# Pools of one PSUM slot each, and modulation sums hung behind named DVE instructions

## The chip, the core and the metric

The kernel runs on one core of one Trainium2 chip. The metric is the device time of one execution in microseconds; lower is better.

## The reference, cut to what matters

Two transformer blocks run one after the other over 1024 tokens of width 1024, all in float32. Each block takes six modulation vectors from a conditioning vector, mixes the tokens, and ends in a gated feed-forward network with a small convolution between its up-projection and its gate.

```python
def first_block(x, c, w_mod, b_mod, ...):
    mod = (silu(c) @ w_mod + b_mod)[:, None, :]
    sh1, sc1, g1, sh2, sc2, g2 = split(mod, 6)
    h = _rms(x, norm1_w) * (1 + sc1) + sh1
    ...                                     # state-space layer and windowed attention
    x = x + g1 * (mixed @ w_out)
    h2 = _rms(x, norm2_w) * (1 + sc2) + sh2
    return x + g2 * _conv_ffn(h2, w_up, conv_w, conv_b, w_down)

def _conv_ffn(h, w_up, conv_w, conv_b, w_down):
    up = causal_depthwise_conv(h @ w_up, conv_w) + conv_b     # width 3, 2 x 2816 columns
    val, gate = split(up, 2)
    return (silu(gate) * val) @ w_down

def second_block(x, c, ctx, c_ctx, ada_w, ada_b, ...):
    mx = split((silu(c) @ ada_w + ada_b)[:, None, :], 6)
    mc = split(silu(c_ctx) @ ada_w + ada_b, 6)
    ...                                     # recurrent, convolutional and spatial mixers
    x_new = layer_norm(ALPHA * x + mx[2] * (mix_x @ w_out), ln1_g, ln1_b)
    ffn_x = conv_ffn(modulate(x_new, mx[3], mx[4]), ffn_up, ffn_conv_w, ffn_conv_b, ffn_down, rows)
    return layer_norm(ALPHA * x_new + mx[5] * ffn_x, ln2_g, ln2_b)
```

`c` is one vector, so a modulation vector is one row times a 1024 x 1024 matrix.

## The kernel before

The products are float32 accuracy out of three reduced ones: each operand is split into a high part (`wh`, `gh`, a cast on ACT) and a low part (`wl`, `gl`, a subtraction on POOL or DVE, line 147 or 143), and three matmuls add high x high, high x low and low x high into one PSUM accumulator.

A planner sets the order of the work. The program is written in one order; the planner simulates it and gives every engine its own queue, in which an instruction stands where its inputs and its buffer are ready in that simulation, earlier written work first. On the chip each queue then runs strictly in that order. Tiles come from pools; a tile with `bufs=n` takes one of n slots when one is free. A pool that is opened over the space of a closed one waits for it.

PSUM has eight banks. `psum` (line 88) opens a set of pools by role and closes the set before; `pt` (line 100) takes a tile of a role. A role in capitals takes two banks a slot (1024 columns), one in small letters one bank. The sets that matter here: up-projection of block 1 `U=2, y=2, v=1, m=1` (line 1307), of block 2 `U=3, y=1, v=1` (line 1693), both down-projections `d=8` (line 1160), the start of block 2 `lv=2, tp=1, o=1` and `z=4` (lines 1315, 1316).

**Up-projection** (`up_proj`, line 1036). 22 pairs p, each a column tile of `val` and the one of `gate` that belongs to it. Pairs 0 to 2 are `plain`: four products of 24 matmuls. Pairs 3 to 21 are `seven` (line 1117): the 2 x 2 block product of a pair with seven half-size products instead of eight, 84 matmuls in all, on sums of weights made by POOL (`prep`, line 1092) and on sums of activations T1 to T4. DVE adds the seven results up, in lines 1126, 1128, 1130, 1133 and 1135, into `gt` (gate half) and back into the PSUM tile U (value half). `act` then runs the convolution of the pair before: in block 1 `gate1` (line 1247; DVE line 1257, ACT line 1255), in block 2 `gate2` (line 1276), and ACT's queue stores the result to DRAM. The raw weights come over SP's queue (line 122) into three buffers.

**Down-projection** (`down_proj`, line 1158). Two column halves; in each, eight accumulators `ps_d`, one for each tile of tokens, take 11 steps q of 48 matmuls (six a tile). `load` (line 1170) brings the weights of a step, multiplies them by the gate row (DVE, line 1175), splits them (POOL), and brings and splits two stored tiles (`gl`, DVE line 147). Steps 0 and 1 of the first half are loaded at high priority and run for six accumulators first and then for the last two; `slots` is the order of the accumulators. At the end of the first half DVE adds each accumulator to the residual (`put`, line 1196), which frees it for the second half.

**Modulation sums.** What the later stages need of the modulation vectors is computed beside the feed-forward network of block 1. `mod_half` (line 287) makes 512 columns of one vector: eight loads of 128 x 512 weights (`mw`, two buffers, SP, line 293) and eight DVE instructions (lines 296 and 298) that add each times its scalar into `macc`. Then small matmuls (lines 209 and 228, into role `m`) sum over the partitions, and DVE adds the bias. It is a generator that yields after each of the eight:

```python
        for k in range(KT):
            t = pool.tile([P, 512], F32, tag="mw", name="mw", bufs=2)
            nc.sync.dma_start(t, self.a[w][k * P:(k + 1) * P, o:o + 512])
            ...
                v.scalar_tensor_tensor(acc, t, s, acc, op0=ALU.mult, op1=ALU.add)
            if k < KT - 1:
                yield
```

`mods_up` makes ten such halves, 80 sums, for the up-projection, which asks for four or five after each pair from the third on (line 1151); `mods_down` makes six halves, 48 sums, and the down-projection asks for three after each `load` (line 1226). Nothing ties a sum to a place but that it is written there.

Of the kernel before, what the change touches and what calls it, by code (L numbers as in the profile page):

```python
# [19 lines left out]
F32 = mybir.dt.float32  # L20
# [4 lines left out]
ALU = mybir.AluOpType  # L25
AX = mybir.AxisListType

P = 128
D = 1024
# [5 lines left out]
PLAIN = 3  # L35
# [30 lines left out]
class Net:  # L66
# [21 lines left out]
    def psum(self, layer=0, **roles):  # L88

        for k in sorted(self.psctx, reverse=True):
            if k >= layer:
                self.psctx.pop(k).close()
        self.psctx[layer] = es = self.es.enter_context(ExitStack())
        for r, n in roles.items():
            pool = es.enter_context(self.tc.tile_pool(name="ps_" + r, bufs=1, space=bass.MemoryType.PSUM))
            self.psn[r] = (pool, n)

    def pt(self, role, *shape):  # L100
        if callable(role):
            return role(*shape)
        n = 1024 if role.isupper() else 512
        pool, bufs = self.psn[role]
        return pool.tile(list(shape) or [P, n], F32, tag=role, name="ps_" + role, bufs=bufs)
# [39 lines left out]
    def split_on(self, eng, hi, lo, x):  # L145
        self.nc.scalar.copy(hi, x)  # L146
        eng.tensor_sub(lo, x, hi.bitcast(F32))  # L147
# [139 lines left out]
    def mod_half(self, w, part, vec, half, acc, pool):  # L287

        nc, v = self.nc, self.nc.vector
        o = part * D + half * 512  # L290
        for k in range(KT):
            t = pool.tile([P, 512], F32, tag="mw", name="mw", bufs=2)
            nc.sync.dma_start(t, self.a[w][k * P:(k + 1) * P, o:o + 512])
            s = self.cact[:, vec * 8 + k:vec * 8 + k + 1]
            if k == 0:
                v.tensor_scalar(acc, t, s, None, op0=ALU.mult)
            else:
                v.scalar_tensor_tensor(acc, t, s, acc, op0=ALU.mult, op1=ALU.add)  # L298
            if k < KT - 1:
                yield  # L300

    def mods_up(self, role):

        for w, part, vec, to, bias in self.MODS_UP:
            for half in range(2):
                acc = self.mpool.tile([P, 512], F32, tag="macc", name="macc", bufs=1)
                yield from self.mod_half(w, part, vec, half, acc, self.mpool)
                self.mod_put(to, half, acc, bias, vec, role)
                yield

    def mods_down(self, accs, pool):

        self.sums = []
        for w, part, vec, to, bias in self.MODS_DOWN:
            for half in range(2):
                acc = accs[:, len(self.sums)]
                self.sums.append((to, half, acc, bias, vec))
                yield from self.mod_half(w, part, vec, half, acc, pool)
                yield
# [715 lines left out]

    def up_proj(self, up, act_fn, g_dr, step, mods):
# [80 lines left out]
        def seven(p):  # L1117
# [8 lines left out]
            v.tensor_add(u2, u2, y)  # L1126
            self.mm_half(z, b, 0, *T3, stop=False)
            v.tensor_add(u4, u2, z)
            self.mm_half(Z, b, 512, *T1, stop=False)
            v.tensor_add(gt[:, 512:1024], u4, Z)  # L1130
            self.mm_half(X, c, 0, *B21, start=False)
            self.mm_half(z, c, 512, *T4, start=False)
            v.tensor_add(gt[:, 0:512], u2, z)
            self.mm_half(Z, d, 0, *B22, start=False)
            v.tensor_add(Z, u2, Z)
# [6 lines left out]
        for p in range(NF):  # L1142
# [8 lines left out]
            for _ in range(4 + p % 2 if p >= PLAIN else 0):  # L1151
                next(step, None)
# [5 lines left out]
    def down_proj(self, down, gate, g_dr, x_dr, setup, done, slots, alpha, mods):  # L1158
# [9 lines left out]
        NQ = NF // 2  # L1168

        def load(nh, q):  # L1170
# [4 lines left out]
            v.tensor_tensor(r2, r2, gh, op=ALU.mult)  # L1175
            self.split_on(nc.gpsimd, *w, r)
            hs = []
            for p in (2 * q, 2 * q + 1):
# [3 lines left out]
                self.split_on(v, h, l, r)  # L1182
# [21 lines left out]
        for nh in range(2):  # L1204
            ps = [self.pt("d") for _ in range(NT)]
            if nh == 0:
# [12 lines left out]
                step = self.mods_down(accs, pool) if mods else iter(())  # L1219
            late = NQ - 3 if nh else NQ  # L1220
            for q in range(0 if nh else 2, late):
# [4 lines left out]
                for _ in range(3):  # L1226
                    next(step, None)
# [588 lines left out]
```

## Time and profile before

| what | value |
|---|---|
| median of 3 runs (lowest, highest) | 2737.31 us (2733.43, 2741.5) |
| the profiled execution: time, span | 2739.78 us, 2737.6 us |
| mean granted clock of TensorE | 0.94 |
| PE busy | 2468.7 us (90%) |
| DVE busy | 1803.5 us (66%) |
| ACT busy | 997.3 us (36%) |
| POOL busy | 1247.3 us (46%) |
| matmuls | 11558 |

The span runs from the first to the last instruction. PE is TensorE, DVE VectorE, ACT ScalarE, POOL GpSimd, SP the engine whose queue issues most transfers. An engine's busy time is the time in which it runs an instruction; what it waits for is named by the engine and line that released it. A clock of 1.00 is the full rate of 2.4 GHz, 0.5 is 1.2 GHz.

### The profile page before, as it was taken

The numbers are of one execution on the slowest core, as the hardware profiler recorded it, in microseconds if no ns is written. First come the engines' busy times: TensorE is split into PE (matmuls) and PEld (weight loads), VectorE is DVE, ScalarE is ACT, GpSimd is POOL, SyncE is SP. The second block draws the span as 40 slices with busy tenths as digits, with TensorE's granted clock in tenths as the row PEclk, the third lists the DMA queues.
The fourth block names the chain that finished last, engine by engine and source line by source line (L and its number), as shares of the span: only waits on it lengthen the run. The fifth ranks groups of instructions, "written<-read, shape, count | busy, mean of one in ns | idle before, by whom it ended". The sixth has DMA issues, their size and how long they took to land.

```text
span 2737.6 us, 31230 instructions
## 1 busy us (share of the span) xinstructions
PE 2468.7 (90%) x11558; PEld 2008.6 (73%) x11558; DVE 1803.5 (66%) x2634; ACT 997.3 (36%) x1470; POOL 1247.3 (46%) x769
## 2 busy tenths in 40 slices
PE   7999989888889979799999878997988999997998
PEld 3777777667768868587777767876766888875886
DVE  8479566877885575645146767677877777775545
ACT  4324543342234432224216446453243333332221
POOL 3353341566667841122123445345345777761222
PEclk9999799999999999899899989999999999998999
DMA  6522124234442256644121101123311222235442
GB/s 240 153 60 59 39 96 189 70 116 146 150 138 74 92 183 217 213 147 145 49 70 54 35 16 51 35 74 117 145 54 61 70 93 78 84 138 185 148 151 86
DMA packets 119017, 295.72 MB, mean 108 GB/s; under 512 B 24145, under 2 KB 38273, under 8 KB 118865
## 3 DMA queue, kind: packets, MB, share of 16 engines
q1 hardware_dynamic: 112528, 270.66, 30.1%
q10 hardware_dynamic: 6336, 23.07, 2.2%
q8 instruction: 91, 1.49, 0.2%
q14 instruction: 62, 0.50, 0.1%
HBM read 243.19 MB, written 49.31 MB: 107 GB/s over the span
## 4 chain that ended last, share of the span: by engine, by line
PE 59%; DVE 20%; DMA 9%; issue 5%; ACT 4%; POOL 3%; SPq 0%; DVEq 0%; POOLq 0%; ACTq 0%
PE ps_d L1192 14%; PE ps_U L1033 11%; PE ps_g L160 8%; PE ps_Z L160 5%; PE ps_v L1033 5%; DMA mw<-in_ada_w 4%; PE ps_z L160 3%; PE ps_y L1033 3%; DVE macc L298 2%; DVE cv L1257 2%; PE ps_lv L1588 2%; DVE cv L1276 1%; DVE gl L147 1%; DVE wl L143 1%; PE ps_s L606 1%
## 5 line engine op out<-in xcount | busy, mean ns | idle before, releaser
L147 POOL TENSOR_TENSOR wl<-wr,wh 128x512 fp32r<-128x512 f32 (+1 forms) x158 | 282.0, 1795 | 543.3 <-ACT wh L146 515.1
L1033 PE MATMUL ps_U<-a,wh 128*128 128x512 f32 x1216 | 386.6, 400 | 12.2 <-ACT u L1124 8.7
L1192 PE MATMUL ps_d<-wh,gh 128*128 128x512 f32 x704 | 278.0, 395 | 53.9 <-DVE cv L1276 24.7
L1033 PEld LDWEIGHTS ps_U<-a,wh 128*128 128x128 f32 x1216 | 233.6, 193 | 63.2 <-ACT u L1124 9.7
L1192 PE MATMUL ps_d<-wh,gl 128*128 128x512 f32 x704 | 276.3, 393 | 3.3 <-DVE gl L147 3.3
L1192 PE MATMUL ps_d<-wl,gh 128*128 128x512 f32 x704 | 277.4, 394 | 0.0
L160 PE MATMUL ps_g<-wh,a 128*128 128x512 f32 (+1 forms) x768 | 245.8, 400 | 25.9 <-ACT wh L141 11.8
L1033 PE MATMUL ps_U<-a,wl 128*128 128x512 f32 x608 | 241.0, 398 | 1.4 <-POOL wl L147 1.4
L160 PE MATMUL ps_Z<-a,wh 128*128 128x512 f32 x704 | 230.4, 405 | 4.6 <-DVE vs L1380 4.6
L1276 DVE SCALAR_TENSOR_TENSOR cv<-ps_U,cols,cv 128x945 f32<-128x945 f32 (+2 forms) x176 | 213.8, 1219 | 27.3 <-ACT cv L1268 24.4
L147 POOL TENSOR_TENSOR wl<-S,wh 128x512 fp32r<-128x512 f32 (+1 forms) x114 | 201.4, 1780 | 32.8 <-ACT wh L146 32.8
L146 ACT CAST gh<-rx 128x1024 fp32r<-128x1024 f32 x88 | 89.4, 1046 | 340.7 <-PE ps_d L1192 130.6
L1192 PEld LDWEIGHTS ps_d<-wh,gh 128*128 128x128 f32 x704 | 134.0, 190 | 83.9 <-issue 55.9
L160 PEld LDWEIGHTS ps_g<-wh,a 128*128 128x128 f32 x768 | 149.4, 202 | 59.6 <-ACT wh L141 12.9
L147 DVE TENSOR_TENSOR gl<-rx,gh 128x1024 fp32r<-128x1024 f32 x88 | 127.6, 1480 | 51.7 <-ACT gh L146 51.7
L160 PEld LDWEIGHTS ps_Z<-a,wh 128*128 128x128 f32 x704 | 134.6, 194 | 31.1 <-issue 5.0
L1192 PEld LDWEIGHTS ps_d<-wh,gl 128*128 128x128 f32 x704 | 133.9, 190 | 31.9 <-DVE gl L147 4.1
L160 PE MATMUL ps_g<-wl,a 128*128 128x512 f32 (+1 forms) x384 | 152.6, 398 | 4.4 <-POOL wl L143 2.9
L143 POOL TENSOR_TENSOR wl<-wr,wh 128x1024 fp32r<-128x1024 f32 x35 | 92.5, 2644 | 140.5 <-ACT wh L141 140.3
L1192 PEld LDWEIGHTS ps_d<-wl,gh 128*128 128x128 f32 x704 | 134.1, 190 | 28.5 <-issue 0.9
L146 ACT CAST wh<-S 128x512 fp32r<-128x512 f32 (+1 forms) x114 | 84.2, 762 | 190.8 <-POOL S L1108 133.2
L146 ACT CAST wh<-wr 128x512 fp32r<-128x512 f32 (+1 forms) x158 | 112.6, 736 | 104.7 <-PE ps_v L1033 36.5
(526 smaller groups left out, 5827.9 us busy)
## 6 DMA issues: line engine op xcount, KB each, us to landing
mw<-in_ada_w SPq DMA_DIRECT2D x112, 256.0 KB
wr<-in_w_up SPq DMA_DIRECT2D x44, 512.0 KB
rx<-g_w_up SPq DMA_DIRECT2D x44, 512.0 KB
wr<-in_f_up SPq DMA_DIRECT2D x44, 512.0 KB
rx<-g_f_up SPq DMA_DIRECT2D x44, 512.0 KB
g_w_up<-cv ACTq DMA_DIRECT2D x22, 512.0 KB
wr<-in_w_down SPq DMA_DIRECT2D x22, 512.0 KB
g_f_up<-cv ACTq DMA_DIRECT2D x22, 512.0 KB
```

Of the source, the lines that this page charges most:

```text
L143: (self.nc.gpsimd if self.turn else self.nc.vector).tensor_sub(lo, x, hi.bitcast(F32))
L146: self.nc.scalar.copy(hi, x)
L147: eng.tensor_sub(lo, x, hi.bitcast(F32))
L160: self.nc.tensor.matmul(out, a, b, start=i == 0, stop=i == n - 1)
L298: v.scalar_tensor_tensor(acc, t, s, acc, op0=ALU.mult, op1=ALU.add)
L606: nc.tensor.matmul(ps[:, gp, 1:P], wc[o:o + 64, r, gp, 1:9].rearrange("p k h -> p (k h)"), st[o:o + 64, r, gp, 0:P - 1], start=False, stop ...
L1033: self.nc.tensor.matmul(out, a, b, start=start and i == 0, stop=stop and i == 11, skip_group_check=True)
L1192: nc.tensor.matmul(ps, a[:, sl], b, start=q == 0 and j == 0, stop=q == NQ - 1 and j == 5, skip_group_check=True)
L1257: v.scalar_tensor_tensor(t[:, s:], us[part][:, :L - s], wt(j), t[:, s:], op0=ALU.mult, op1=ALU.add)
L1276: v.scalar_tensor_tensor(ov, s[:, r0 + di:r1 + di, c0 + dj:c1 + dj], wt(3 * (di + 1) + dj + 1), ov, op0=ALU.mult, op1=ALU.add)
L1588: nc.tensor.matmul(ps[:, j], ck(kk)[:, j], ck(qq)[:, j], start=True, stop=True)
```

## The change

Three things are changed. `psum` opens n pools of one slot for a role of n slots, and `pt` takes them in turn. `mod_half` loads the weights of sum k+1 right after it has written sum k, one step ahead of their use, and yields ahead of each sum; the extra yields of its callers go. And the generator is no longer advanced after a pair or a load: `behind` advances it right after one DVE instruction is written and tells the planner that what this puts on DVE may not be queued ahead of that instruction (it sets no wait, and it does not bind transfers, ACT or PE). The instructions are the four adds of each pair, a fifth in every fourth pair, and in the down-projection the weight product and the two `gl` of each `load`.

```diff
@@ def psum
         for r, n in roles.items():
-            pool = es.enter_context(self.tc.tile_pool(name="ps_" + r, bufs=1, space=bass.MemoryType.PSUM))
-            self.psn[r] = (pool, n)
+            self.psn[r] = cycle([es.enter_context(self.tc.tile_pool(name=f"ps_{r}{j}", bufs=1, space=bass.MemoryType.PSUM))
+                                 for j in range(n)])
@@ def pt
-        pool, bufs = self.psn[role]
-        return pool.tile(list(shape) or [P, n], F32, tag=role, name="ps_" + role, bufs=bufs)
+        return next(self.psn[role]).tile(list(shape) or [P, n], F32, tag=role, name="ps_" + role, bufs=1)
@@ def mod_half
+        def load(k):
+            t = pool.tile([P, 512], F32, tag="mw", name="mw", bufs=2)
+            nc.sync.dma_start(t, self.a[w][k * P:(k + 1) * P, part * D + half * 512:part * D + half * 512 + 512])
+            return t
+
+        t = load(0)
         for k in range(KT):
-            t = pool.tile([P, 512], F32, tag="mw", name="mw", bufs=2)
-            nc.sync.dma_start(t, self.a[w][k * P:(k + 1) * P, o:o + 512])
+            yield
             s = self.cact[:, vec * 8 + k:vec * 8 + k + 1]
             if k == 0:
                 v.tensor_scalar(acc, t, s, None, op0=ALU.mult)
             else:
                 v.scalar_tensor_tensor(acc, t, s, acc, op0=ALU.mult, op1=ALU.add)
             if k < KT - 1:
-                yield
+                t = load(k + 1)
@@ def mods_up, def mods_down
-                yield
@@ new
+    def behind(self, ins, step):
+
+        with self.tc.issue_after(ins.ins):
+            next(step, None)
@@ def seven
-            v.tensor_add(u2, u2, y)
+            self.behind(v.tensor_add(u2, u2, y), step)
             self.mm_half(z, b, 0, *T3, stop=False)
-            v.tensor_add(u4, u2, z)
+            self.behind(v.tensor_add(u4, u2, z), step)
             self.mm_half(Z, b, 512, *T1, stop=False)
-            v.tensor_add(gt[:, 512:1024], u4, Z)
+            self.behind(v.tensor_add(gt[:, 512:1024], u4, Z), step)
...
-            v.tensor_add(gt[:, 0:512], u2, z)
+            self.behind(v.tensor_add(gt[:, 0:512], u2, z), step)
             self.mm_half(Z, d, 0, *B22, start=False)
-            v.tensor_add(Z, u2, Z)
+            ins = v.tensor_add(Z, u2, Z)
+            if p % 4 == 0:
+                self.behind(ins, step)
@@ the loop over pairs
-            for _ in range(4 + p % 2 if p >= PLAIN else 0):
-                next(step, None)
@@ def load, in down_proj
-            v.tensor_tensor(r2, r2, gh, op=ALU.mult)
+            self.behind(v.tensor_tensor(r2, r2, gh, op=ALU.mult), step)
...
-                self.split_on(v, h, l, r)
+                self.behind(self.split_on(v, h, l, r), step)
@@ the loop over steps
-                for _ in range(3):
-                    next(step, None)
```

## Rows read from the trace of the kernel before

**Rows 1.** Busy time by stretch: us, each engine's busy time (instructions), clock, DMA share, GB/s.

```profile
core 0: us, PE busy (x) PEld busy (x) DVE busy (x) ACT busy (x) POOL busy (x), PEclk, DMA share, GB/s
577.90:829.70 251.80, 218.07 (x909) 174.97 (x909) 203.04 (x190) 76.51 (x101) 161.31 (x98) 0.93 0.43 142
829.70:982.90 153.20, 153.20 (x674) 125.90 (x673) 84.20 (x81) 62.64 (x80) 124.23 (x80) 1.00 0.24 79
...
1018.00:1128.80 110.80, 110.80 (x480) 91.60 (x481) 63.69 (x61) 25.21 (x25) 20.92 (x8) 0.98 0.66 219
1128.80:1160.80 32.00, 11.62 (x49) 8.71 (x48) 20.58 (x23) 6.08 (x6) 4.78 (x2) 0.81 0.61 199
...
2114.20:2437.90 323.70, 323.70 (x1430) 268.11 (x1429) 237.02 (x239) 115.74 (x154) 237.03 (x170) 1.00 0.24 80
...
2483.60:2490.00 6.40, 6.33 (x15) 5.01 (x16) 1.23 (x1) 1.06 (x1) 0.00 (x0) 0.51 0.29 97
2490.00:2693.00 203.00, 203.00 (x897) 168.12 (x897) 89.33 (x68) 53.28 (x55) 52.82 (x18) 1.00 0.44 147
```

**Rows 2.** Groups of DVE's instructions, 577.9 to 829.7: count, busy, mean ns, idle before.

```profile
L298 DVE SCALAR_TENSOR_TENSOR macc<-mw,cact,macc 128x512 f32<-128x512 f32 x66 | 83.1, 1259 | 38.2 <-DMA mw<-in_ada_w 30.8 <-DMA mw<-in_w_mod 6.8
...
L296 DVE TENSOR_SCALAR macc<-mw,cact 128x512 f32<-128x512 f32 x9 | 7.6, 840 | 0.0
```

**Rows 3.** What PE waited for, 577.9 to 829.7: us in total, times, longest.

```profile
PE ps_m L209 <- DVE macc L298: 14.6, 5, 4.1
PE ps_U L1033 <- ACT u L1124: 8.7, 3, 4.6
```

**Rows 4.** Groups of PE's instructions, 577.9 to 829.7: the sums' own matmuls.

```profile
L209 PE MATMUL ps_m<-ones,macc 128*128 128x1 f32 x64 | 9.0, 252 | 14.6 <-DVE macc L298 14.6
...
L228 PE MATMUL ps_m<-macc,ones 128*1 128x512 f32 x4 | 2.0, 590 | 0.0
```

**Rows 5.** Timeline at the first down-projection's start, DVE and PE: start, us, instruction, idle before.

```profile
1001.66 3.48 DVE L147 TENSOR_TENSOR gl<-rx,gh 128x1024 fp32r<-128x1024 f32 x3
...
1016.51 1.27 DVE L1257 SCALAR_TENSOR_TENSOR cv<-ps_U,cols,cv 128x1022 f32<-128x1022 f32 x1
...
1017.93 0.77 PE L1192 MATMUL ps_d<-wh,gh 128*128 128x512 f32 x1 [12.13 <-DVE cv L1257]
```

**Rows 6.** Timeline at the second down-projection's start, DVE and PE.

```profile
2456.24 2.34 DVE L147 TENSOR_TENSOR gl<-rx,gh 128x1024 fp32r<-128x1024 f32 x2
...
2468.18 1.22 DVE L147 TENSOR_TENSOR gl<-rx,gh 128x1024 fp32r<-128x1024 f32 x1
...
2477.22 6.29 DVE L1276 SCALAR_TENSOR_TENSOR cv<-ps_U,cols,cv 128x1008 f32<-128x1008 f32 x5
...
2483.66 0.76 PE L1192 MATMUL ps_d<-wh,gh 128*128 128x512 f32 x1 [24.66 <-DVE cv L1276]
```

**Rows 7.** What PE waited for, 1115 to 1180.

```profile
PE ps_d L1192 <- DVE a L1201: 17.1, 1, 17.1
```

**Rows 8.** Timeline of DVE inside the first down-projection: two sums.

```profile
1111.01 1.90 DVE L298 SCALAR_TENSOR_TENSOR a<-mw,cact,a 128x512 f32<-128x512 f32 x1 [1.77 <-DMA mw<-in_ada_w]
...
1125.46 2.42 DVE L298 SCALAR_TENSOR_TENSOR a<-mw,cact,a 128x512 f32<-128x512 f32 x2 [5.38 <-DMA mw<-in_ada_w]
```

**Rows 9.** Timeline at the start of block 2, DVE, ACT and PE.

```profile
1299.63 1.22 DVE L143 TENSOR_TENSOR wl<-wr,wh 128x1024 fp32r<-128x1024 f32 x1
...
1309.01 0.56 ACT L380 ACTIVATE hT<-ps_d,mod_sh_a,mod_sc_a 128x256 f32<-128x256 f32 x1 [0.32 <-PE ps_d L379]
...
1309.97 0.78 PE L160 MATMUL ps_z<-wh,a 128*128 128x512 f32 x1
```

**Rows 10.** Groups of DVE's instructions, 1018 to 1160.8: the sums of line 298.

```profile
L298 DVE SCALAR_TENSOR_TENSOR a<-mw,cact,a 128x512 f32<-128x512 f32 x42 | 38.5, 916 | 48.1 <-DMA mw<-in_ada_w 47.7
```

**Rows 11.** Timeline of PE ahead of pair 0 of block 1.

```profile
496.42 0.48 PE L379 MATMUL ps_s<-ident,xn 128*128 128x128 f32 x1 [7.00 <-DVE xn L348]
```

**Rows 12.** What SP's queue waited for, 829.7 to 982.9.

```profile
SPq L122 <- POOL wl L147: 148.6, 15, 19.6
```

More of the change, by code (lines that the diff above doesn't have):

```diff
@@ L146, in split_on @@
         self.nc.scalar.copy(hi, x)
-        eng.tensor_sub(lo, x, hi.bitcast(F32))
+        return eng.tensor_sub(lo, x, hi.bitcast(F32))
     def gate_row(self, i):
@@ L289, in mod_half @@
         nc, v = self.nc, self.nc.vector
-        o = part * D + half * 512
+        def load(k):
[3 more added lines that the diff above has]
+        t = load(0)
         for k in range(KT):
-            t = pool.tile([P, 512], F32, tag="mw", name="mw", bufs=2)
-            nc.sync.dma_start(t, self.a[w][k * P:(k + 1) * P, o:o + 512])
+            yield
             s = self.cact[:, vec * 8 + k:vec * 8 + k + 1]
@@ L318, in mods_down @@
                 yield from self.mod_half(w, part, vec, half, acc, pool)
-                yield
     def mods_end(self, ps):
@@ L1168, in down_proj @@
         NQ = NF // 2
+        step = iter(())
         def load(nh, q):
@@ L1218, in down_proj @@
                     accs = self.act.tile([P, KT, 512], F32R, tag="a16", name="a16", bufs=4).bitcast(F32)
-                step = self.mods_down(accs, pool) if mods else iter(())
+                    step = self.mods_down(accs, pool)
             late = NQ - 3 if nh else NQ
```

## The prediction

> **What bounds the kernel now.** I read the busy time by stretch first, then what DVE and PE wait for where PE is not full, then the timelines at the edges. In most stretches PE is never idle at a granted clock of 1.00: eight late pairs of the first up-projection take 153.2 us, 19.15 a pair, and 17 pairs of the second block's 19.04 each [rows 1]. So time can be won only where PE stands, and the change touches four such places.
>
> First, the ten pairs before those eight (from pair 3 on, where `seven` begins, 84 matmuls each) take 251.8 us, 25.2 a pair, PE busy 218.1 at clock 0.93 [rows 1]. What sets them apart is the modulation sums: 75 of the 80 that the first up-projection does run here (66 on line 298, 9 on line 296), 90.7 us of DVE, and DVE stands 37.6 us for their weights [rows 2]. With 203.0 us busy [rows 1] that is 240.6 of 251.8: DVE is the bound. In the eight late pairs it is busy 84.2 us, 10.5 a pair [rows 1]. The generator is asked for 4 or 5 sums a pair, but the planner, for which a load has landed sooner than it does, issues 7.5. PE's own waits are the consequence: 14.6 us of the sums' matmuls for the sum, 8.7 for ACT's copy of the first product, which stands behind DVE's convolution [rows 3].
>
> Second, between the first up-projection and its down-projection PE stands 12.13 us, released by DVE's last read of pair 21's U (line 1257, start 1016.51) [rows 5]. By the addresses of the kernel before, the accumulator that is written first lies in bank 0, which pair 20 held and left 20 us earlier; so the one pool of eight waits as a whole. The same edge in block 2 costs 24.66 us [rows 6], and then 6.4 us at clock 0.51 [rows 1]. Third, inside the first down-projection 32.0 us pass with 49 matmuls, where 10.9 would do (203.0/897 x 48) [rows 1]: PE waits 17.1 us for DVE's evacuation of line 1201 [rows 7], which is queued behind weight products and sums that wait up to 5.4 us for a load [rows 8]. Fourth, the first `z` of block 2 starts at 1309.97, when ACT has read the last `ps_d` (1309.01 plus 0.56) [rows 9].
>
> **The change part by part.** Nothing is computed more or less: sums, loads, matmuls and evacuations keep their number and change their place.
>
> *Sums in the up-projection.* 81 calls of the generator hang on the 81 places that the 19 pairs offer, 4 or 5 a pair. DVE's demand becomes 10.5 + 90.7/19 = 15.3 us of 19.15; in the late pairs it was idle 8.6 a pair, so 4.8 go into 8.6. Behind each sum on DVE stand the next add, which frees `z` for PE, and the convolution; block 2 runs such pairs with DVE 13.9 of 19.04 busy and PE full [rows 1]. The next load leaves a whole step before its sum; with two `mw` buffers it waits only for the sum before the last, and so has two steps, some 9 us, to land. DVE's waits for a load were 5.4 us at most [rows 8], so the 37.6 go. Ten pairs then cost 10 x 19.15 = 191.5, plus the sums' own matmuls, 11.0 in this stretch [rows 4], plus some stall, since a half ends ten times and PE may come early to its matmul. Its bounds: none, or all that PE idles today but for those waits, 33.7 - 14.6 = 19.1. I take 6, nearer to none, as the other waits too come from a late DVE. Gain 251.8 - 208.5 = 43 (30 to 49).
>
> *First edge.* With a pool a bank the first product needs bank 0 alone. Late next is DVE's `gl`: three ended at 1005.14 [rows 5]. The last pair now has four sums among these, 1.26 each [rows 2], 5 us: start 1010 instead of 1017.9, and 1 us less at the low clock. Gain 9; bounds 3 (DVE, fully busy here, delays `gl` by ten) and 14 (no delay, clock kept).
>
> *Sums in the down-projection.* Three a step of 10.9 us behind the weight product and the two `gl`, where 48 ran in the first twelve steps (42 on line 298 [rows 10]). DVE needs 1.4 + 2 x 1.3 + 3 x 0.9 = 6.7 us a step. The third sum's load can leave only when the first has freed its buffer, some 3 us before, so it may wait 2.4: 9.1 still fits. The 21.1 us go; I leave 3 for the evacuations at the turn of halves. Gain 18 (8 to 21).
>
> *Edge into block 2.* `z` needs four split weights, the last done at 1300.85 [rows 9], and a bank that was evacuated before. The transposes still share PE. From 1310 to 1304: gain 6 (0 to 9).
>
> *Second edge.* Free banks let step 0 start when PE is done, at 2459.0. Its two `gl` are ready at 2458.6, the fourth only at 2469.4 [rows 6]: step 0 on six tiles fills 8.2 us, then 2.1 of waiting, 8.2 for step 1, and at 2477.7 the last two tiles wait for the convolution, whose run of five ends at 2483.5: 5.8 more. Of 24.7 + 3.2 (half of 6.4 at half clock) 20 remain. Bounds 28 (later steps go ahead meanwhile) and 10 (the order on DVE gets worse).
>
> *The rest.* `y` of pair 0 may run in the 7.0 us that PE waits for the last normalisation [rows 11], but pair 0 is soon held by DVE and ACT again: 1 (0 to 5). Slots go round in written order where they went to the first one free; in the mixers a slow holder can block a user: 0, bounds 5 lost and 3 won.
>
> Sum: 43 + 9 + 18 + 6 + 20 + 1 = 97. The profiled execution took 2739.8 us (span 2737.6), so 2642.8; it lies 2.5 above the median of the runs, 2737.3, so **2640 us**.
>
> **The rivals.** *POOL stretches the sums.* Line 298 took 1259 ns in the ten pairs, POOL busy 64% of the time [rows 1, 2], and 916 in the down-projection, POOL busy 19% [rows 1, 10]. The late pairs, into which sums now move, have POOL at 81% [rows 1]. If each sum took 1.9 us (the slowest of [rows 8]), DVE would need 10.5 + 4.2 x 1.9 = 18.5 a pair, and if half of its present idle time, 4.3, is waiting for PE that nothing fills, a pair takes 22.8: 433 us for 19, no gain in the up-projection. Time 2683. Against it: the convolution is already stretched in the 10.5. The Trainium skill, GPSIMD Engine Reference, section 1 (Specifications), says that GpSimd shares its SBUF interfaces with VectorE and contends with DVE instructions that have two SBUF inputs, as the sum has; by that rule the sums get dearer where they go. The two means above agree with it.
>
> *The pools change nothing.* The trace names no banks. If the first product waited for something else that ended with the last convolution, both edges and `z` stay and only the sums gain: 43 + 18 = 61, 2676. For it: in block 2 that read is the natural release. Against: in block 1 it is not.
>
> *The sums do not stay where they are hung.* Each may not come before its add, but it may come later; if the planner lets half of them gather as before, 30 of the 61 are lost: 2670.
>
> *SP's queue turns it slower.* In the late pairs SP stood 148.6 us for POOL to free raw weights, up to 19.6 at once [rows 12]. If one load of a sum stands behind such a wait in every pair, it leaves 19.6 late and takes up to 5.4 to land; with 9 of lead DVE waits 16.0, has 3.8 to spare, and a pair takes 12.2 more: 232 us, 2870. Above 97/19 = 5.1 us a pair the change is slower. Against: the planner orders SP by when it holds a buffer to be free, so a raw load should stand behind the sums' loads, not ahead.
>
> **How the numbers follow.** Forecast 0.60; POOL's stretch 0.13; pools without effect 0.11; sums gathered 0.08; SP's queue 0.05; the gains eaten by a new order elsewhere 0.03. All terms at their best give 134 us (49 + 14 + 21 + 9 + 28 + 5 + 3, plus 5 if the sums' matmuls hide), so 2603; at their worst 46, so 2691; the first three rivals (2670 to 2683) lie between. Range 2605 to 2692: outside are SP's queue, the eaten gains and the forecast's own misses, under 0.2. A difference of 0.3% is about what a measurement of this kernel can tell from none. Faster by more: 0.92; within it: 0.03; slower by more: 0.05.
>
> **What would show it.** Right: all 19 pairs near 19.7 us; DVE's waits for `mw` under 5 us in the up-projection; the first product of each down-projection ahead of the last read of U; no stretch of 32 us inside the first; `z` ahead of the last read of `ps_d`. Wrong: pairs over 21 us with sums above 1.5 us, or with `mw` loads on SP behind a wait for POOL; PE's gaps at the two edges unchanged; the mixers (to 400 us, and 1310 to 1860) longer by over 5 us.

## The result, and the profile after

| | before | after |
|---|---|---|
| median of 4 runs each, us | 2735.37 (2723.45 to 2741.5) | 2635.05 (2632.64 to 2656.5) |
| profiled execution: time, span, us | 2739.78, 2737.6 | 2632.81, 2630.4 |
| mean granted clock of TensorE | 0.94 | 0.955 |
| PE, DVE, POOL busy, us | 2468.7, 1803.5, 1247.3 | 2454.8, 1816.2, 1260.8 |

The changed kernel takes 0.9656 of the time before (95% interval 0.9595 to 0.9717): 100 us less, where 97 were forecast. The two traces differ by 107.2 us. Read from the first matmul of each stage in both, this is where they went (milestones of the stages; minus is gained):

| stretch | before | after | change | forecast |
|---|---|---|---|---|
| up to the first matmul of `seven` | 577.9 | 588.9 | **+11.0** | 0 (3 gained to 5 lost), pair 0: -1 |
| 19 pairs of block 1 | 427.9 | 385.2 | -42.7 | -43 (-30 to -49) |
| first edge | 12.1 | 5.6 | -6.5 | -9 (-3 to -14) |
| first down-projection | 272.0 | 252.5 | -19.5 | -18 (-8 to -21) |
| from there to the first `ps_Z` | 130.4 | 114.7 | **-15.7** | -6 (0 to -9) |
| `ps_Z` to the second `seven` | 669.9 | 666.8 | -3.1 | 0 |
| 19 pairs of block 2 | 368.7 | 365.8 | -2.9 | 0 |
| second edge, down-projection and end | 278.6 | 250.8 | -27.8 | -20 (-10 to -28) |

The first view of the changed kernel is busy time by stretch, with the columns of [rows 1]: the pairs with sums in two parts, then the last pair, the first down-projection up to the turn of its halves, and the turn.

```profile
588.90:784.00 195.10, 193.08 (x847) 156.26 (x847) 160.97 (x142) 77.51 (x101) 169.39 (x100) 1.00 0.41 136
784.00:948.10 164.10, 161.55 (x728) 132.78 (x727) 140.46 (x125) 61.73 (x80) 139.95 (x81) 1.00 0.39 131
948.10:973.80 25.70, 21.26 (x85) 17.07 (x84) 22.74 (x22) 9.32 (x11) 13.08 (x6) 0.87 0.45 153
979.80:1091.60 111.80, 111.80 (x482) 92.34 (x483) 72.29 (x65) 33.14 (x33) 24.78 (x9) 0.98 0.74 264
1091.60:1104.30 12.70, 11.07 (x49) 8.88 (x49) 7.21 (x9) 3.05 (x3) 2.45 (x1) 1.00 0.66 230
```

Where ten pairs had DVE as their bound at 25.2 us [rows 1], 18 pairs now take 359.2 us, 19.96 each, with PE busy 99% of it at the full clock and DVE 84% (16.7 us a pair; 10.5 + 4.2 x 1.45, the mean of the next fence, makes 16.6). The turn of halves takes 12.7 us instead of 32.0.

The groups of DVE in the 18 pairs (count, busy, mean ns, idle before), which answer [rows 2]:

```profile
L301 DVE SCALAR_TENSOR_TENSOR macc<-mw,cact,macc 128x512 f32<-128x512 f32 x65 | 93.9, 1445 | 0.5 <-DMA mw<-in_w_mod 0.5
...
L299 DVE TENSOR_SCALAR macc<-mw,cact 128x512 f32<-128x512 f32 x10 | 7.9, 794 | 0.0
```

And what PE waited for there (us, times, longest), which answers [rows 3]:

```profile
PE ps_U L1034 <- DVE cv L1262: 2.3, 2, 1.9
PE ps_U L1034 <- POOL wl L146: 1.4, 1, 1.4
PE ps_m L208 <- DVE macc L301: 0.4, 1, 0.4
PE ps_v L1034 <- DVE u L1134: 0.2, 1, 0.2
```

DVE's wait for the sums' weights fell from 37.6 us to 0.5, and PE's wait for the sums from 14.6 to 0.4. A sum itself got dearer: 1445 ns instead of 1259. The timelines of DVE and POOL ahead of the last pair show when. The first sum runs beside a split of POOL; the second falls into a gap of POOL, which lasts until 949.43:

```profile
943.91 3.00 DVE L301 SCALAR_TENSOR_TENSOR macc<-mw,cact,macc 128x512 f32<-128x512 f32 x1
943.93 2.44 POOL L146 TENSOR_TENSOR wl<-S,wh 128x1024 fp32r<-128x1024 f32 x1
...
947.44 0.74 DVE L301 SCALAR_TENSOR_TENSOR macc<-mw,cact,macc 128x512 f32<-128x512 f32 x1
949.43 4.14 POOL L146 TENSOR_TENSOR wl<-wr,wh 128x512 fp32r<-128x512 f32 x2 [3.07 <-ACT wh L145]
```

All 70 sums of line 301 in the 19 pairs, sorted so by this trace (in which POOL's spans are rough): 5 found POOL idle throughout and took 741 ns on average, 46 lay wholly beside POOL's instructions and took 1308, 19 partly, 1899. In the kernel before, 29 of 69 found POOL idle, at 747 ns. So the sums got dearer because fewer of them now find POOL idle.

The timeline of PE at the first edge and at the start of block 2 (start, us, instruction, idle before), which answers [rows 5, 9]:

```profile
963.58 0.80 PE L1034 MATMUL ps_v<-T4h,wh 128*128 128x512 f32 x1 [4.44 <-DVE u L1134]
...
979.77 0.80 PE L1199 MATMUL ps_d<-wh,gh 128*128 128x512 f32 x1 [4.85 <-ACT gh L145]
...
1231.87 0.40 PE L1199 MATMUL ps_d<-wh,gl 128*128 128x512 f32 x1
1232.11 0.27 PE L380 MATMUL ps_d<-ident,rx 128*128 128x128 f32 x1
1232.22 0.27 PE L380 MATMUL ps_d<-ident,xn 128*128 128x128 f32 x1
1232.25 0.48 PE L159 MATMUL ps_z<-wh,a 128*128 128x512 f32 x1
```

The first product of the down-projection no longer waits for a read of U; it waits for the cast of its stored tile. What SP's queue waited for between 955 and 980 says why that came late:

```profile
SPq L1187 <- PE ps_m L208: 4.8, 1, 4.8
SPq L1187 <- DVE macc L301: 4.7, 1, 4.7
```

The loads of those tiles (line 1187, issued at 974.95) wait for the last readers of the sums: the `rx` tiles come free only with them. At block 2, `z` begins 0.4 us after the start of the last product of the down-projection and fills the gaps between the transposes, which had PE to themselves for 20 us before.

The timeline of PE at the second edge, which answers [rows 6]:

```profile
2379.15 0.39 PE L1034 MATMUL ps_U<-a,wl 128*128 128x512 f32 x1
2379.38 0.39 PE L1199 MATMUL ps_d<-wh,gh 128*128 128x512 f32 x1
2379.60 0.39 PE L1199 MATMUL ps_d<-wl,gh 128*128 128x512 f32 x1
...
2381.19 0.39 PE L1199 MATMUL ps_d<-wh,gl 128*128 128x512 f32 x1
```

No gap is left, and no half clock behind it. Eight products that need no `gl` run first; which step a product belongs to, the trace does not name.

### The profile page after: what moved, and what is told of

The parts are those of the page before. It is cut to its first block, busy times and chain, and to the rows that moved or that the text cites. A ratio compares the mean times of both kernels' runs of the same rounds, so it can differ in the third digit from the quotient of the medians.

```text
span 2630.4 us, 31222 instructions
## 1 busy us (share of the span) xinstructions
PE 2454.8 (93%) x11558; PEld 1996.0 (76%) x11558; DVE 1816.2 (69%) x2634; ACT 1002.2 (38%) x1473; POOL 1260.8 (48%) x769
## 4 chain that ended last, share of the span: by engine, by line
PE 65%; DVE 16%; DMA 6%; issue 5%; POOL 4%; ACT 4%; SPq 0%; POOLq 0%; ACTq 0%; DVEq 0%
PE ps_d L1199 15%; PE ps_U L1034 13%; PE ps_g L159 7%; PE ps_v L1034 7%; PE ps_Z L159 5%; PE ps_z L159 4%; PE ps_y L1034 3%; PE ps_lv L1593 2%; DVE cv L1262 1%; DMA wr<-in_w_down 1%; PE ps_s L607 1%; DVE wl L142 1%; DMA a<-in_w_mod 1%; PE ps_s L159 1%; DMA wr<-in_w_out 1%
## 5 line engine op out<-in xcount | busy, mean ns | idle before, releaser
L146 POOL TENSOR_TENSOR wl<-wr,wh 128x512 fp32r<-128x512 f32 (+1 forms) x158 | 291.7, 1858 | 446.6 <-ACT wh L145 446.6
L1034 PE MATMUL ps_U<-a,wh 128*128 128x512 f32 x1216 | 375.3, 390 | 3.9 <-DVE cv L1262 2.3
L1199 PE MATMUL ps_d<-wh,gl 128*128 128x512 f32 x704 | 270.5, 389 | 0.0
L1034 PEld LDWEIGHTS ps_U<-a,wh 128*128 128x128 f32 x1216 | 227.4, 188 | 53.2 <-issue 6.7
L159 PE MATMUL ps_g<-wh,a 128*128 128x512 f32 (+1 forms) x768 | 243.6, 395 | 17.1 <-ACT wh L140 11.7
L1281 DVE SCALAR_TENSOR_TENSOR cv<-ps_U,cols,cv 128x945 f32<-128x945 f32 (+2 forms) x176 | 213.5, 1218 | 27.4 <-ACT cv L1273 24.7
L146 POOL TENSOR_TENSOR wl<-S,wh 128x512 fp32r<-128x512 f32 (+1 forms) x114 | 213.3, 1886 | 20.1 <-ACT wh L145 19.4
L1199 PEld LDWEIGHTS ps_d<-wh,gl 128*128 128x128 f32 x704 | 132.3, 188 | 27.4
```

What stands on the lines that cost most here:

```text
L146: return eng.tensor_sub(lo, x, hi.bitcast(F32))
L159: self.nc.tensor.matmul(out, a, b, start=i == 0, stop=i == n - 1)
L1034: self.nc.tensor.matmul(out, a, b, start=start and i == 0, stop=stop and i == 11, skip_group_check=True)
L1199: nc.tensor.matmul(ps, a[:, sl], b, start=q == 0 and j == 0, stop=q == NQ - 1 and j == 5, skip_group_check=True)
L1281: v.scalar_tensor_tensor(ov, s[:, r0 + di:r1 + di, c0 + dj:c1 + dj], wt(3 * (di + 1) + dj + 1), ov, op0=ALU.mult, op1=ALU.add)
```

## The experiments

Twelve kernels, each against the kernel before. A ratio is of this kernel to that one. "Start of `seven`" is the time of the first matmul of line 1034 in a kernel's trace.

### The pools alone

```diff
 (the kernel before)
-            pool = es.enter_context(self.tc.tile_pool(name="ps_" + r, bufs=1, space=bass.MemoryType.PSUM))
-            self.psn[r] = (pool, n)
+            self.psn[r] = cycle([es.enter_context(self.tc.tile_pool(name=f"ps_{r}{j}", bufs=1, space=bass.MemoryType.PSUM))
+                                 for j in range(n)])
...
+        return next(self.psn[role]).tile(list(shape) or [P, n], F32, tag=role, name="ps_" + role, bufs=1)
```

> The kernel before with the PSUM pools alone changed; the sums stay as they were. Theory (pools and sums act apart): the edges and z gain what the changed kernel shows there (6.5 us at the first edge, 15.8 from the last ps_d matmul to the first Z, 24.8 at the second edge, some 9 in the later stages), and the stages ahead of line 1033's first matmul get 11 longer, since the slots of the mixers go round: 2735 - 56 + 11 = 2690 us, the ten pairs at 25 us each as before. Rival 1 (the 11 us come from the sums' new order): the first line-1033 matmul stays at 578 us, 2679 in all. Rival 2 (the pools' edges only gain when the sums leave DVE free there): first edge stays at 12 us or more, 2700 or above.

2680.05 us, ratio 0.9783 (0.9745 to 0.9821). The start of `seven` is at 589.3, the first edge gains 12.3 us (to none), the stretch up to `ps_Z` 15.7, the second edge with its down-projection 27.4; 19 pairs take 430.4, as before. So the pools earn all three edges, and the 11 us ahead of `seven` come with them. The first edge gains twice what the whole change shows there: with the sums gone from the last pairs, as they are here, the `rx` tiles are free early.

### The sums alone

```diff
 (the changed kernel)
-            self.psn[r] = cycle([es.enter_context(self.tc.tile_pool(name=f"ps_{r}{j}", bufs=1, space=bass.MemoryType.PSUM))
-                                 for j in range(n)])
+            pool = es.enter_context(self.tc.tile_pool(name="ps_" + r, bufs=1, space=bass.MemoryType.PSUM))
+            self.psn[r] = (pool, n)
...
+        return pool.tile(list(shape) or [P, n], F32, tag=role, name="ps_" + role, bufs=bufs)
```

> The changed kernel with the shared pools put back, the sums as changed. Theory (they act apart): pairs at 20.3 us each, 385 us for 19 (gain 42.7), the first down-projection 19.5 shorter, both edges and z as before (12, 25 and 20 us), `seven` starting at 578: 2735 - 62 = 2673. Rival (the turn of the halves in the first down-projection was shortened by the pools): the down-projection stays at 271 us and the turn at 32, so 2735 - 43 = 2692. Second rival (the slots are not what makes the stages before `seven` longer): `seven` starts at 589 here too, 2684.

2679.52 us, ratio 0.9782 (0.975 to 0.9814). 19 pairs take 382.5 (gain 45.4), the first down-projection 256.5 (gain 15.5), PE's wait at the turn falls from 17.1 to 5.1; the second edge stays at 24.7 us and `z` at 20.1. `seven` starts at 567.7, ten earlier than before, though nothing ahead of it was changed: the clock there differs from execution to execution (below), and this profiled execution (2664.38) lies 15 us under the median. Each half by itself gives 58 us, 116 in all, 16 more than the change; 9.5 of these are the first edge, which gains 12.3 in the one, 3.7 in the other and 6.5 with both.

### The sums without the lead, and the lead without the tie

```diff
 (the first: the changed kernel, mod_half)
-        t = load(0)
         for k in range(KT):
             yield
+            t = load(k)
...
-            if k < KT - 1:
-                t = load(k + 1)
```

```diff
 (the second: the changed kernel)
 def behind
-        with self.tc.issue_after(ins.ins):
-            next(step, None)
+        pass
 the loop over pairs
+            for _ in range(4 + p % 2 if p >= PLAIN else 0):
+                next(step, None)
 the loop over steps
+                for _ in range(3):
+                    next(step, None)
```

> The changed kernel, but each load of the sums written at its own step again, right ahead of its sum; the sums still queued behind the given DVE instructions. Theory (the place on DVE earns the gain; the load is not bound by it, so the planner still sends it when a buffer is free): 2635 to 2650 us, DVE's waits for mw in the 18 pairs under 15 us in all. Rival (the lead earns it): each of the 80 loads leaves at its add and takes 2 to 5 us to land, in which DVE's queue stands; pairs at 22 us or more, DVE's waits for mw over 60 us in all, 2680 us or more.

> The changed kernel, with the loads one step ahead, but the sums written after each pair (4 or 5) and each load of the down-projection (3) as before, and tied to no DVE instruction. Theory (the tie earns the gain): the sums gather in the first ten or eleven pairs again, those at 24 to 25 us, and the turn of the halves at 25 us or more: 2690 us, 2635 + 55. Rival (the lead earns it): DVE's 37.6 us of waiting for mw go, the ten pairs fall to 20.5 us although the sums gather, and the time is 2640 to 2655.

Without the lead: 2630.97 us, ratio 0.9604 (0.9571 to 0.9638), the same as the changed kernel. Without the tie: 2681.49 us, ratio 0.9793 (0.9752 to 0.9834), all of the sums' gain gone. The groups of DVE in the pairs with sums, first without the lead (588 to 948), then without the tie (600 to 855):

```profile
L301 DVE SCALAR_TENSOR_TENSOR macc<-mw,cact,macc 128x512 f32<-128x512 f32 x65 | 93.5, 1439 | 0.7 <-DMA mw<-in_w_mod 0.7
```

```profile
L301 DVE SCALAR_TENSOR_TENSOR macc<-mw,cact,macc 128x512 f32<-128x512 f32 x69 | 80.4, 1166 | 45.2 <-DMA mw<-in_ada_w 32.4 <-DMA mw<-in_w_mod 12.3
```

The tie alone takes DVE's waits for the weights away; the lead alone takes none of them away. With the lead, the sums still gather in ten pairs of 22.4 to 27.1 us, and 45.2 us go in waiting. A load is bound to no DVE instruction, so it leaves when its buffer is free, lead or not; what it needs is that the sums stand apart.

### Shared pools in the mixers

```diff
 (the changed kernel)
+            own = r in ("U", "y", "v", "m", "d", "z")
+            ps = [es.enter_context(self.tc.tile_pool(name=f"ps_{r}{j}", bufs=1, space=bass.MemoryType.PSUM))
+                  for j in range(n if own else 1)]
+            self.psn[r] = (cycle(ps), 1 if own else n)
```

> The changed kernel, with pools of one slot for the roles U, y, v, m, d and z alone; s5, g, tp, lv, o and Z (the mixers) share one pool a role as before. Theory (the slots in written order put PE at half clock in the mixers of block 1: 0.50 between 250 and 300 us in three runs with such pools, 0.85 and 0.90 in two without): the mixers run at over 0.8 in that stretch, the last transposes end near 490 to 500 us instead of 516 to 519, the plain pairs stay as long as in the changed kernel, and the whole takes 2612 to 2625 us. Rival (that stretch falls by chance, whatever the pools): 0.50 there again, 2630 to 2640. Second rival (Z, tp and g of block 2 gain from the pools, too): the block-2 mixers lose 4 or more against the changed kernel.

2637.03 us, ratio 0.9637 (0.9614 to 0.9659): missed, nothing was gained. `seven` starts at 580.8, 8 us earlier than in the changed kernel, but block 2 gave it back, as the second rival had it: 118.6 us up to `ps_Z` instead of 114.7, 236.3 from the end of `ps_Z` to the second `seven` instead of 231.3, 368.8 for the pairs instead of 365.8. So the next kernel shares the pools of s5, g and tp in block 1's mixers alone (the condition `own` becomes: no role s5 in the call).

> The changed kernel, with one pool a role as before for the mixers of block 1 alone (s5, g, tp); pools of one slot everywhere else, block 2's mixers among them. Theory (in block 1's mixers slots in turn cost 8 to 10 us, by the clock; in block 2's they gain 11: z to Z 4, Z to the second pairs 5 to 7, pairs 3, all of which the run with roles shared in both lost): line 1034's first matmul at 578 to 583 instead of 589, everything behind it as in the changed kernel, 2625 to 2628 us. Rival (the mixers of block 1 differ from run to run by their clock, not by the pools): 586 to 592, 2632 to 2637.

2620.32 us, ratio 0.9595 (0.956 to 0.963). `seven` starts at 579.9, and every stretch behind it is within some 2 us of the changed kernel's. The kernel before ran at 2726.97 us here, 0.3% lower than beside the changed kernel; by the ratio to that median it is 2625, which is the theory's figure. The interval overlaps with the changed kernel's.

### ACT's copy ahead of the casts

```diff
 (the changed kernel)
+                ins = nc.scalar.copy(gt[:, n * 512:n * 512 + 512], gs[n])
+                if p == 0:
+                    self.cp = ins
...
+                with self.tc.issue_after(self.cp.ins):
+                    sums()
```

> The changed kernel, with the instructions of sums() that go to ACT tied behind ACT's copy of the first v of pair 0. Theory (in the plain pairs, 83 to 85 us with the new pools and 78 with the old, PE stands 8.5 us at the second v because that copy is queued behind casts of T2 that wait 16.8 us for DVE): the gap goes and the plain pairs take 76 to 79 us, 2635 - 6 = 2629. Rival (the time is DVE's: sums of activations and convolutions of the pairs before hold the next product anyway): the gap moves to a later v or U and the plain pairs stay at 82 to 85, 2635.

2635.12 us, ratio 0.9626 (0.9594 to 0.9657): the plain pairs did fall from 82.9 to 77.6 us, but the 19 pairs took 390.5 instead of 385.2. The timeline of PE in this run shows the wait in two new places:

```profile
568.21 1.19 PE L159 MATMUL ps_U<-a,wh 128*128 128x512 f32 x2 [6.54 <-DVE cv L1265]
602.77 0.50 PE L1034 MATMUL ps_y<-T2h,wh 128*128 128x512 f32 x1 [3.59 <-ACT wh L145]
```

In the changed kernel the copy of the first v is queued behind ACT's cast of T2, which waits 16.8 us for DVE, and PE stands 8.5 us for it. With the copy first, a convolution of DVE and a cast of weights on ACT end the next waits, the second of them in the first pair of `seven`, which takes 24.8 us instead of 20.7: the time moved and stayed, as the rival said.

### The last pair and the first edge

Five sums in every odd pair, so that the last pair has none:

```diff
 (the changed kernel)
-            if p % 4 == 0:
+            if p % 2:
                 self.behind(ins, step)
```

> The changed kernel, with the fifth sum of a pair in every odd pair instead of every fourth, so that the sums end in pair 20 and the last pair has none. Theory (the four sums of the last pair stretch it and delay the adds, the gl and the loads of the first edge): the last pair falls from 25.7 to 20 to 22 us and the first edge from 5.6 to 2 or less, 2635 - 7 = 2628; the other pairs get 0.2 longer each at most. Rival (the last pair and the edge are held by the loads of the first two steps, which the sums do not touch): the two stay at 31 us together, 2633 to 2637. Second rival (five sums in every second pair are more than fit): pairs at 21 us, 2645.

2641.39 us, ratio 0.9647 (0.9621 to 0.9672). Last pair and edge fell from 31.3 to 24.8 us (25.0 and -0.2, as the products of both stages mix), nearly what the theory asked. But 19 pairs took 403.7 instead of 385.2: pairs of 22.7 to 27.3 us among others of 19 to 21, in which PE waited 10.8 us for POOL's splits (1.4 in the changed kernel). Why POOL came late was not isolated. Nor did the edge's gain reach the end of the stage: edge and first down-projection together took 258.0 us, and 258.1 in the changed kernel.

Seventy of the 80 sums left out:

```diff
 (the changed kernel, mod_half)
+        n = 1 if pool is self.mpool else KT
-        for k in range(KT):
+        for k in range(n):
```

> The changed kernel, with seven of the eight sums of each half left out in the up-projection (70 of 80, and their loads); the modulation rows that it makes there are then those of the first 128 inputs alone. Theory (what is left of the sums' cost is little: their own matmuls, 8.7 us, stay, and 20.3 a pair against 19.15 leaves at most 1.1 x 19 = 21, of which 8.7 are those matmuls): 19 pairs at 374 to 378 us instead of 385, 2625. Rival (GpSimd stretches sums and adds, 1445 ns a sum, and they hold the pairs): pairs fall to 19.1 and the last to 20, 365 us or less, and the edge shrinks, 2608 or below.

2624.2 us, ratio 0.9594 (0.9565 to 0.9623). 19 pairs take 379.3 us, 5.9 less than in the changed kernel, and the edge 5.8 less. So seventy sums, some 100 us of DVE at 1445 ns, cost the pairs 6 us and the edge 6. The edge's 6 do not reach the end of the stage: edge and first down-projection together take 258.0 us here, too. Another 7.7 us of this trace's gain lie ahead of `seven` (581.2 instead of 588.9), where nothing was left out. Busy time of this run over the 19 pairs (PE, PE's loads, DVE, ACT, POOL):

```profile
581.20:960.40 379.20, 374.87 (x1665) 307.05 (x1664) 228.29 (x220) 153.96 (x194) 291.04 (x186) 1.00 0.28 94
```

POOL's work is the same, 186 instructions here and 187 in the changed kernel, yet it was busy 291.0 us here and 322.4 there (169.39 + 139.95 + 13.08): the sums stretch POOL's instructions, and, by the sorted sums above, POOL theirs.

### Sums moved into the down-projection

```diff
 (the changed kernel)
-               ("ada_w", 1, 1, "sc_a", "ab1"), ("ada_w", 1, 2, "sc_a", "ab1")]
-    MODS_DOWN = [("ada_w", 2, 1, 2, "ab2"), ("ada_w", 3, 1, "sh_b", "ab3"), ("ada_w", 4, 1, "sc_b", "ab4")]
+               ("ada_w", 1, 1, "sc_a", "ab1")]
+    MODS_DOWN = [("ada_w", 1, 2, "sc_a", "ab1"), ("ada_w", 2, 1, 2, "ab2"), ("ada_w", 3, 1, "sh_b", "ab3"), ("ada_w", 4, 1, "sc_b", "ab4")]
...
-                self.behind(self.split_on(v, h, l, r), step)
+                ins = self.split_on(v, h, l, r)
+                self.behind(ins, step)
                 hs.append((h, l))
+            self.behind(ins, step)
```

> The changed kernel, with the last 16 of the up-projection's 80 sums (sc_a of the second vector) made in the down-projection, which has a fourth place after each load; so the last three pairs have no sums. Theory (the last pair and the first edge, 25.7 + 5.6 us, are held by the sums among their adds and gl; the down-projection has DVE to spare, three sums cost it nothing on PE): last pair and edge together at 23 to 25 instead of 31, the down-projection the same within 2, 2628 us. Rival (four sums a step are too many for the two mw buffers, and the evacuations at the turn of the halves come late): the edge gains 6, the first half of the down-projection loses 6 or more, 2635 or above.

> The two before together. Theory (they act apart): 2635 - 8 - 7 = 2620 us. Rival (the clock in the mixers is chance, and the sums only move the wait): 2630 to 2635.

Moved: 2628.67 us, ratio 0.9628 (0.9596 to 0.9659). Last pair and edge are 22.6 us instead of 31.3, but the first down-projection took 263.0 instead of 252.5; theory and rival both came about and cancel. With block 1's mixers shared as well: 2614.0 us, ratio 0.9582 (0.9547 to 0.9616). What is lost in the down-projection is PE's wait at the turn of the halves in that run:

```profile
PE ps_d L1203 <- DVE a L1212: 11.0, 1, 11.0
```

The last kernel moves half as many, and has the fourth place a step only behind the turn:

```diff
 (mixers of block 1 shared, as above)
-            for half in range(2):
+            for half in range(1 if (part, vec) == (1, 2) else 2):
...
-        for w, part, vec, to, bias in self.MODS_DOWN:
-            for half in range(2):
+        for w, part, vec, to, bias in self.MODS_DOWN + self.MODS_UP[-1:]:
+            for half in range(1 if vec == 2 else 0, 2):
...
+            if nh:
+                self.behind(ins, step)
```

> As the run with both, but only the last 8 of the up-projection's 80 sums go to the down-projection, and its fourth place a step is in the second half alone. Theory (what the down-projection lost with 16 more, 7 us up to its last step of the first half and 3 behind it, came of four sums a step ahead of the turn, where PE stood 11.0 us): the last pair and the edge stay short (22 to 23 us, no gap), the first half is back at 124 to 127 us, and the time is 2605 to 2610. Rival (the turn is late for another reason, as a run with no sum more in the down-projection showed 129.5 us there, too, once PE came into it earlier): 128 to 131 again, 2612 to 2616.

**2610.16 us, ratio 0.9555 (0.9524 to 0.9587)**, the lowest median of all. Its interval lies below the changed kernel's, but overlaps with those of the run that shares block 1's mixers alone (0.956 to 0.963) and of the run with both moves (0.9547 to 0.9616). In the traces, 14.6 of the 20.2 us between it and the first of these lie ahead of `seven`, where both have the same mixers. Last pair and edge are at 19.1 us. The first half of the down-projection takes 128.6 us, in the rival's range (124.1 in the changed kernel, 131.4 with all sixteen moved): PE waits 8.8 us at the turn there, with three sums a step as in the changed kernel, so the place of the fourth was the smaller part of the loss. With the first edge gone, the turn is late without a fourth sum, too: the two runs without that edge and with no sum more in the down-projection (five sums in every odd pair, seventy left out) wait 8.8 and 9.7 us there, where the changed kernel waits 1.6. Edge and down-projection together take 257.9 to 258.0 us in these three, 258.1 in the changed kernel, and 259.4 to 264.0 in four others that keep the edge and the sums' places (without the lead, with shared mixers in one block or both, with ACT's copy first). So what the edge gives up comes back at the turn in part or in full; why was not isolated. The loads of the first stored tiles leave while the pairs still run, which end at 945.2 (SP's timeline):

```profile
929.64 1.28 SPq L1189 DMA_DIRECT2D rx<-g_w_up  x3
```

In the changed kernel they left at 974.95, after the end of the pairs at 974.1.

## Why the prediction was right, and where it was not

**Sums in the up-projection: right in size, wrong in one cause.** 43 foretold, 42.7 in the traces, 45.4 for the sums alone. That DVE was the bound because the sums gathered, and that 4.2 a pair fit into its idle time, is shown by the run without the tie, in which they gather again and the gain is gone. But the step "the next load leaves a whole step before its sum ... so the 37.6 go" named the wrong cause: without the lead the waits are as small (0.7 us). The mechanism was the place of the sums, and not their loads; that the forecast was right in size although it relied on the lead is luck, since the change made both. The stall was put at 6 us in ten pairs; PE waited 4.3 in 18.

**POOL's stretch: there, and nearly harmless.** The rival asked for 1.9 us a sum to hold the pairs; 1.445 was measured. The Trainium skill, GPSIMD Engine Reference, section 1 (Specifications), says that GpSimd shares its SBUF interfaces with VectorE and contends with DVE instructions that have two SBUF inputs. The traces agree: a sum takes 741 to 747 ns with POOL idle and 1308 to 1899 beside it. They add the other side: POOL was 31 us longer busy with the sums. Spread beside a POOL that is busy 86% of the time (309.3 of 359.2 us in the changed kernel), the sums took 1404 to 1465 ns in nine kernels (1322 in the tenth, with five in every odd pair), gathered ones 1166 to 1259 in three. Leaving out 70 of them gained 6 us in the pairs, so DVE had the room.

**First edge: right.** 9 foretold with 5 us of delay by the sums of the last pair; 6.5 in the traces, 12.3 where those sums are gone. What delays is not mainly `gl` behind sums on DVE, as the text had it, but the loads of the stored tiles, which wait for the sums' last readers. That the edge counts by itself was too simple: where it is gone, the turn of halves takes much of the time back (above).

**Sums in the down-projection: right.** 18 against 19.5; the sums alone give 15.5 and the pools alone 6.5. The turn is still the weak place: PE stands there under 2 us in the changed kernel and 11.0 in the run with both moves. One reading was off: the longest wait of DVE for a load in that stretch was 7.0 us and not the 5.4 of [rows 8], which shows only part of it. With 7.0 the third sum would wait 4.0, and DVE's step of 10.7 us would fit only just into 10.9.

**Start of block 2: the term was too small, and its bound too low.** 6 (0 to 9) against 15.7. The step that failed is "`z` needs four split weights, the last done at 1300.85": it needs one to begin, and with a bank of its own it runs between the transposes. They left PE 7.6 of 20.5 us idle in the kernel before, at a clock of 0.64.

**Second edge: near its upper bound.** 20 (10 to 28) against 27.4. The two waits subtracted, 2.1 for the fourth `gl` and 5.8 for the last two banks, did not come: PE has no gap in this stretch. The text had given the bound's reason, that later steps go ahead meanwhile; which products went ahead cannot be read from the trace.

**"In the mixers a slow holder can block a user: 0, bounds 5 lost and 3 won": wrong by 11 us.** The prediction's own sign for it, mixers longer by over 5 us, came. The pools alone lose them, and sharing the pools of block 1's mixers brings 8 to 9 back (14 between the run that moved sixteen sums and the one that did both). What failed is the mechanism, a slow holder that blocks a user: ahead of pair 0 PE stands 55.8 us in the kernel before and 49.9 in the changed one, so it does not wait longer. Its clock is lower, 0.71 instead of 0.83 between 240 and 350 us (next section but one). Since executions with the same mixers also differ there by 10 us, the size of the loss is uncertain. In block 2 pools of one slot win 9 us, by the run that shared the mixers of both blocks against the changed kernel (3.9 + 5.0 + 3.0, less 2.9 that `ps_Z` itself is longer). That the forecast of the whole came out within 5 us is in part luck, of errors that cancel: 11 us lost that it did not know, against 17 more at the edges into block 2 and its down-projection and 6 in block 2 than it had counted.

**The other rivals** fell: that the pools change nothing, with their run alone; that the sums would not stay where they hang, with 19 to 22 us for all pairs but the last; that SP's queue would bring the loads late, with 0.5 us of waiting for them.

## What to carry to other kernels

Where a helper's work is spread by the order of writing, count in the trace where it really lands; tying each piece to an instruction on its own engine's queue moved 75 sums out of ten pairs and was worth 45 us, and loading earlier was worth nothing. At a change of stage ask which single buffer the first instruction needs and which pool makes it wait for all the others; and treat pools of one slot as a choice for each stage, since they win where one stage takes over from another and can lose inside one.

## What the runs showed of the hardware that was not expected

In block 1's mixers the granted clock of TensorE goes with the pools, and differs between executions of the same mixers, too. Between 240 and 350 us PE was busy 101 to 106 us in all 14 kernels, but the granted clock was 0.52 to 0.74 in the eight with pools of one slot there (0.71 in the changed kernel), and 0.77 to 0.94 in the six with shared pools (0.83 before, 0.94 in the fastest). `seven` started at 581 to 601 us in the eight and at 565 to 581 in the six. Each of the 14 is a single execution. PE's busy time by stretch in the run with the pools alone (us, busy, instructions, clock, DMA share, GB/s):

```profile
228.00:234.00 6.00, 6.00 (x30) 1.00 0.05 8
234.00:240.00 6.00, 3.78 (x22) 0.89 0.49 169
240.00:318.00 78.00, 75.95 (x302) 0.50 0.14 31
318.00:324.00 6.00, 6.00 (x44) 1.00 0.01 3
```

PE stood for 2.2 of 6 us, fell from 2.4 to 1.2 GHz, and stayed there for 78 us although it was busy for 76 of them. So a high busy share is no sign of a high clock: in the 110 us from 240 on, PE was busy 106.2 us with 428 matmuls at a clock of 0.52 (the run without the tie), and 101.1 us with 643 at 0.94 (the fastest kernel). What brings the clock back, as at 318 us in these rows, is not shown: from 270 to 306 us PE was busy all the time in this run and stayed at 0.50. Executions with the same mixers differ here too: 0.83 in the kernel before and 0.94 in the run with the sums alone, which are 10 us apart at the start of `seven`, so much of the spread between runs may come from here. Why slots in turn go with the lower clock, and which of the three roles does it, was not tried.
